# The output projection by seven half-size products, its first token half completed two products ahead, with norms by two and four tiles

## The chip, the cores and the metric

The kernel runs as one program on one core of a Trainium2 chip. The engines named here are PE (TensorE, matmuls; PEld is its weight load), DVE (VectorE), ACT (ScalarE), POOL (GpSimd) and SP (SyncE, which starts most transfers). The metric is the device time of one execution in microseconds. Three runs of the kernel before took 1897.14, 1898.09 and 1899.58 us; the median is 1898.09.

## The reference

A residual block over 1024 tokens of width 1024 in float32: two attention-like branches are merged by gates, projected by `w_out`, normalised and added to `x`; then comes an MLP with squared ReLU. The part around the change:

```python
merged = jax.nn.sigmoid(m_a) * y_a + jax.nn.sigmoid(m_d) * y_d
x = x + gate1 * rms_norm(merged @ w_out, post_mix_w)

h2 = rms_norm(x, pre_mlp_w) * (1.0 + scale2) + shift2
y = jnp.square(jax.nn.relu(h2 @ mlp_w1)) @ mlp_w2
x = x + gate2 * rms_norm(y, post_mlp_w)
```

`merged @ w_out` is 1024 x 1024 x 1024. Each RMS norm needs a sum of squares over all 1024 columns of a token, and `h2` is needed with features on the partitions, so that every token tile is transposed on PE.

## The kernel before

**Products in three matmuls.** A float32 operand is split into a high part (a cast, on ACT) and a low part (the difference, on DVE). A product is high x high, high x low and low x high: three matmuls of 128x128 by 128x512 for each 128 features.

**Seven products of halves.** The two branches' projections ahead of this stage are 1024-wide too, and each is done by seven products of half-size blocks (Strassen's way, with sums and differences of blocks formed on DVE). A half-size product is 4 token tiles x 4 feature tiles x 3 = 48 matmuls. The three of the branches are `ga`, `md` and `gd`; the reads of `gd`'s products in `gdn_read` finish the merged `z`, four tiles `zf(tb, kp)` for each half of the tokens with features on partitions. They need the gates from DRAM, loaded into tiles named `sl`.

**w_out before.** The eight token tiles are projected one after the other: for each, 8 feature tiles x 3 x 2 column halves = 48 matmuls into one `pm` tile (128x1024 in PSUM, two such in use by turns), 384 in all. `m_high`/`m_low` split the merged `z`; `wo_load`, `wo_high`, `wo_low` load and split `w_out`, whose low parts come for six of the eight feature tiles from a negated copy on ACT and an accumulating transfer that POOL starts.

**After a token tile** `token_chain` (lines 1794 to 1835) runs: ACT squares the `pm` tile with a sum into `cv`; DVE multiplies by the gain `gw1` into `z`; `norm1` is ten small operations on one column (a reciprocal root by iteration) and the residual into `xr`; ACT squares `xr`; `norm2` is again ten small operations and a scaling into `xh`; then `tr` has PE transpose `xh` in eight 128x128 pieces, by four into a `pa` tile, and ACT writes them, scaled and shifted, as `F`, the MLP's input.

**What sets the order.** A clock of ticks. In this stage a tick is six matmuls. `at(dt, fn)` puts a function on an agenda, due `dt` ticks ahead (`st` counts from the start of the branches), and `tick()` issues what is due behind the last matmul. After this each engine executes its instructions strictly in the order of issue (class `InOrder`, through whose `call` on line 38 they all go, so that every row of the profile shows L38 and tiles are told by their names). An instruction waits by semaphores for the tiles it touches; a write into a PSUM tile waits for earlier readers of that tile.

In `token_chain` `norm1` is due one tick after the tile, `norm2` four ticks, the output transfer six, the transposes nine and ten; the tile itself takes eight. Pass 1 of the MLP follows (`prod1`, 12 matmuls for each entry of `PASS1`); it needs `F` of the first half of the features split by `split_op`, and its weights' parts `w1`, prepared two entries ahead on ACT and DVE by `prep_pass1`. Sums of `F` for the second pass come through `todo`, filled 13 ticks into pass 1.

Of the kernel before, what the change touches and what calls it, by code (L numbers as in the profile page):

```python
# [8 lines left out]
F32 = mybir.dt.float32  # L9
# [41 lines left out]
def block_kernel(ctx: ExitStack, tc: tile.TileContext, x, c, ada_w, ada_b, pre_mix_w, post_mix_w,  # L51
# [1412 lines left out]
    def pair_tile(p, tag="w4", dt=F32):  # L1464
        return t4((128, 2, 512), dt, p, tag)
# [217 lines left out]

# [3 lines left out]
    def gdn_read(p, ps, h):  # L1687
# [5 lines left out]
        elif p == "P1":  # L1693
# [4 lines left out]
            at(13 - h, lambda: m_high(0, h))  # L1698
            at(16 - 3 * h, lambda: m_low(0, h))
        elif p == "P4":  # L1700
            s_ = gd.s.pop((1, 0, h))
            V.scalar_tensor_tensor(s_, s_, 1.0, pv, add, mul)
            z_add(0, 2 + h, s_)
            at(9 - 2 * h, lambda: m_high(0, 2 + h))
            at(14 - 3 * h, lambda: m_low(0, 2 + h))
        else:
            cb = int(p == "P5")
            y = u["P7" if cb else "P6", h]
            tt(V, y, pv, y, add)
            V.scalar_tensor_tensor(y, gd.s.pop((cb, 1, h)), 1.0, y, add, mul)  # L1710
            z_add(1, 2 * cb + h, y)
            n = 2 * (1 - cb) + h
            at((20, 20, 14, 12)[n], lambda: m_high(1, 2 * cb + h))
            at((22, 22, 16, 14)[n], lambda: m_low(1, 2 * cb + h))

    def branch(b, read):

        ps = None
        for p in ORDER:
# [7 lines left out]
    wo, wraw = [None] * 8, {}

    def wo_load(k, ring):
        if ring:  # L1730
            raw = rp.tile([128, 2, 1024], F32, tag="raw", name=nm("raw"))
            DMA.dma_start(raw, w_out[k * 128:(k + 2) * 128, :].rearrange("(k p) c -> p k c", p=128))
            wraw[k], wraw[k + 1] = raw[:, 0, :], raw[:, 1, :]
        else:
            for i in (k, k + 1):
                wraw[i] = t4(p="wor", tag="hd")
                DMA.dma_start(wraw[i], w_out[i * 128:(i + 1) * 128, :])

    def wo_high(k, tag):
        wo[k] = [t4((128, 1024), F32R, "wO", tag) for _ in range(2)]  # L1740
        A.copy(wo[k][0], wraw[k])

    def wo_low(k, dma=False):
        H, L = wo[k]
        if dma:
            A.activation(L, H.bitcast(F32), AF.Copy, scale=-1.0)
            G.dma_start(L, w_out[k * 128:(k + 1) * 128, :], accum_op=ALU.add)
        else:
            tt(V, L, wraw[k], H.bitcast(F32), sub)
# [44 lines left out]
    def token_chain(t, ps, xr):  # L1794

        hf, to = t // 4, slice(t % 4 * 128, t % 4 * 128 + 128)
        z, xh = t4(p="z", tag="hd"), t4(p="xh", tag="hd")
        v, v2 = small(1, "cv"), small(1, "cv")
        s = {}

        def norm1():
            V.tensor_scalar(v, v, 1.0 / D, 4 * EPS, ALU.mult, ALU.add)
            r = rsqrt(v, 1)
            V.scalar_tensor_tensor(xr, z, r, xr, ALU.mult, ALU.add)
            dump("x1", xr, lambda y: y[t * 128:(t + 1) * 128, :])
# [75 lines left out]


    xrs = {0: load_x(0)}
    for t in range(NT):
        hf, to = t // 4, (t % 4) * 128
        ps = pmt()
        if t + 1 < NT:
            at(7, lambda t=t: xrs.__setitem__(t + 1, load_x(t + 1)))
        if t == 4:
            load_pass1(0)
            load_pass1(1)
        if t == 5:  # L1900
            at(6, lambda: split_op("B11", F[0][0:2], (0,)))
            at(7, lambda: split_op("B11", F[0][0:2], (1,)))
            load_pass1(2)
            load_pass1(3)
        if t == 6:
            at(6, lambda: split_op("B21", F[0][2:4], (0,)))
        if t == 7:
            prep_pass1(0, 0, 3)
            prep_pass1(1, 0, 4)
            at(6, lambda: split_op("B21", F[0][2:4], (1,)))  # L1910
        for k in range(8):
            H, L = mH[k // 2][hf][:, k % 2, to:to + 128], mL[k // 2][hf][:, k % 2, to:to + 128]
            for (lh, w_) in ((H, 0), (H, 1), (L, 0)):
                for cf in range(2):
                    last["pe"] = T.matmul(ps[:, cf * 512:(cf + 1) * 512], lh, wo[k][w_][:, cf * 512:(cf + 1) * 512],
# [456 lines left out]
```

## Time and profile before

| what | value |
|---|---|
| time, median of 3 runs | 1898.09 us |
| the profiled execution's own time | 1896.27 us |
| its span | 1894.5 us |
| granted clock of TensorE, mean | 0.998 |
| first matmul on w_out | 1175.8 us into the span |
| last start of a matmul on w_out | 1268.3 us |
| transposes of `xh` | 64, from 1198.9 to 1283.9 us |
| DVE and ACT busy in 1176 to 1268.5 us | 62.5 and 43.3 us |

The profile is one execution. Its times are microseconds from the start of the span; a matmul's end is modelled, and matmuls overlap, so that the distance from one start to the next is what one costs. A row of the view by time gives start, duration, engine, line, operation, out<-in, shapes and count, and in brackets the engine's idle time ahead of it with what ended it. A row of groups gives the busy sum and the mean in ns after the bar. The view by tile gives smallest, median and largest duration in ns, and first and last start.

### The profile page before, as it was taken

What the parts mean: (1) busy time and instruction counts of PE and PEld (TensorE: products, weight loads), DVE (VectorE), ACT (ScalarE), POOL (GpSimd) and SP (SyncE); (2) the same over time, 40 slices, a digit from 0 to 9 for tenths busy, and PEclk for the clock granted to TensorE, in tenths of its full rate; (3) what the DMA queues carried; (4) which work ended last, traced back from release to release, by engine and by line L of the source; (5) the groups of instructions that cost most, each with busy time, mean ns of one, the idle gap of its engine ahead of it and who ended that gap; (6) DMA issues with size and microseconds to landing.
All of it is one profiled execution on the core that took longest, in us unless ns stands there. A gap on an engine that the chain in (4) does not pass through costs nothing.

```text
span 1894.5 us, 26553 instructions
## 1 busy us (share of the span) xinstructions
PE 1872.8 (99%) x10217; PEld 1572.3 (83%) x10217; DVE 1350.9 (71%) x2178; ACT 883.7 (47%) x1613; POOL 150.2 (8%) x140
## 2 busy tenths in 40 slices
PE   7999999999999999999999999999999999999998
PEld 5788888989898888888888888888888888888886
DVE  6664834968767666766788688666588777677887
ACT  5564324252332444444664556467544446433333
POOL 2120111010110000000101001000022220000001
PEclk9999999999999999999999999999999999999999
DMA  9695573223125444444868758336666768262425
GB/s 320 217 249 185 157 145 101 68 89 112 56 80 164 133 134 126 142 132 130 246 179 213 225 142 233 111 103 213 218 211 223 243 207 315 78 222 98 169 101 100
DMA packets 251567, 312.23 MB, mean 165 GB/s; under 512 B 72530, under 2 KB 178208, under 8 KB 251440
## 3 DMA queue, kind: packets, MB, share of 16 engines
q1 hardware_dynamic: 221936, 274.67, 45.3%
q0 software_dynamic: 13232, 20.85, 6.1%
q10 hardware_dynamic: 16272, 15.02, 2.4%
q8 instruction: 80, 1.31, 0.3%
q14 instruction: 47, 0.39, 0.1%
HBM read 230.10 MB, written 80.39 MB: 164 GB/s over the span
## 4 chain that ended last, share of the span: by engine, by line
PE 96%; DMA 1%; DVE 1%; ACT 1%; issue 0%; DVEq 0%; SPq 0%; ACTq 0%; POOLq 0%
PE pm L38 63%; PE pa L38 33%; DMA wq<-in_w_branch_gla_dram 1%; DMA x<-in_x_dram 0%; ACT hH L38 0%; ACT xT L38 0%; DVE rt L38 0%; ACT ob L38 0%; DVE ya L38 0%; DVE xT L38 0%; DVE rs L38 0%; ACT jk L38 0%; DVE hL L38 0%; DVE wL L38 0%; DVE raw L38 0%
## 5 line engine op out<-in xcount | busy, mean ns | idle before, releaser
L38 PE MATMUL pm<-hH,wH 128*128 128x512 f32 x864 | 286.3, 412 | 0.0
L38 PE MATMUL pm<-hL,wH 128*128 128x512 f32 x864 | 268.7, 392 | 0.0
L38 PE MATMUL pm<-hH,wL 128*128 128x512 f32 x864 | 267.2, 390 | 0.0
L38 PE MATMUL pm<-oH,wB 128*128 128x512 f32 x672 | 214.5, 394 | 0.0
L38 PE MATMUL pa<-w,yH 128*128 128x512 f32 (+1 forms) x696 | 212.3, 387 | 0.0
L38 PEld LDWEIGHTS pm<-hH,wL 128*128 128x128 f32 x864 | 162.1, 188 | 36.4
L38 PEld LDWEIGHTS pm<-hL,wH 128*128 128x128 f32 x864 | 162.2, 188 | 36.1
L38 DVE TENSOR_TENSOR w<-raw,w 128x512 fp32r<-128x512 f32 (+1 forms) x144 | 125.7, 875 | 49.6 <-ACT w L38 48.5
L38 PEld LDWEIGHTS pm<-hH,wH 128*128 128x128 f32 x864 | 145.1, 190 | 17.1 <-issue 0.2
L38 PEld LDWEIGHTS pa<-w,yH 128*128 128x128 f32 x696 | 130.1, 188 | 26.9 <-DVE ya L38 0.4
L38 PEld LDWEIGHTS pm<-oH,wB 128*128 128x128 f32 x672 | 126.2, 188 | 25.9 <-DMA wB<-in_w_branch_gla_dram 0.3
L38 ACT CAST w<-raw 128x512 fp32r<-128x512 f32 (+1 forms) x144 | 99.3, 711 | 89.3 <-DVE raw L38 79.5
L38 PE MATMUL pa<-w,yL 128*128 128x512 f32 (+1 forms) x348 | 134.5, 387 | 0.0
L38 PE MATMUL pm<-oL,wB 128*128 128x512 f32 x336 | 130.9, 390 | 0.0
L38 PE MATMUL pa<-oB,w 128*128 128x512 f32 x480 | 111.4, 390 | 0.0
L38 ACT CAST wH<-raw 128x1024 fp32r<-128x1024 f32 x62 | 64.5, 1048 | 98.1 <-PE pm L38 55.8
L38 PEld LDWEIGHTS pa<-oB,w 128*128 128x128 f32 x480 | 89.8, 188 | 18.5
L38 DVE SCALAR_TENSOR_TENSOR cv<-pm,ccol,cv 128x1023 f32<-128x1023 f32 (+2 forms) x72 | 92.1, 1279 | 13.4 <-ACT cv L38 12.0
L38 DVE TENSOR_TENSOR wL<-raw,wH 128x1024 fp32r<-128x1024 f32 x62 | 75.3, 1219 | 34.6 <-ACT wH L38 34.5
L38 PE MATMUL pm<-oT,w 128*128 128x512 f32 x384 | 90.8, 389 | 0.0
L38 PE MATMUL pa<-oT,w 128*128 128x512 f32 x384 | 90.8, 389 | 0.0
L38 DVE TENSOR_TENSOR ya<-pa,ya 128x512 f32<-128x512 f32 (+1 forms) x83 | 55.9, 682 | 43.7 <-PE pa L38 43.7
(378 smaller groups left out, 3701.1 us busy)
## 6 DMA issues: line engine op xcount, KB each, us to landing
yL<-y_d SPq DMA_DIRECT2D x53, 512.0 KB, 7.6
raw<-in_mlp_w_dram SPq DMA_DIRECT2D x23, 1024.0 KB, 6.2
raw<-in_w_in_dram SPq DMA_DIRECT2D x18, 1024.0 KB, 7.2
raw<-in_w_in_dram SPq DMA_DIRECT2D x32, 512.0 KB, 4.9
araw<-in_ada_w_dram SPq DMA_DIRECT2D x32, 512.0 KB, 3.8
raw<-in_mlp_w_dram SPq DMA_DIRECT2D x18, 512.0 KB, 5.1
araw<-in_ada_w_dram SPq DMA_DIRECT2D x32, 256.0 KB, 6.5
sl<-sg_d SPq DMA_DIRECT2D x16, 512.0 KB, 8.9
```

The costliest lines, as they stand in the source:

```text
L38: r = fn(*args, **kw)
```

## The change

The projection becomes seven half-size products, P2, P1, P6, P5, P3, P7, P4, of 48 matmuls or eight ticks each, over halves of tokens, features and columns; 336 matmuls. `out_product` runs one: four token tiles j, each with four feature tiles. P2 has its own two `pm` tiles; P1, P6, P5 and P3 accumulate onto a second pair, read in between by `copy_y` or `first_half`; P7 and P4 accumulate in four `pa` tiles, with `add_y` after each. A `pm` tile now holds the 512 columns of two token tiles. Tokens 0 to 511 are complete after P3 (tick 40 of the stage), tokens 512 to 1023 after P4 (tick 56).

The loads and sums of blocks stand in a table with ticks (`out_plan`), and all low parts are made on DVE. `token_chain` is gone. `square` works on 128x512; the gain is multiplied on DVE for the first half's second columns (`second_half`) and on POOL for the rest (`weigh`). `norm1` takes two tiles at a time in the first half (ticks 38 and 42) and four in the second (64), `norm2` likewise (42 and 47; 71). `turn` has PE transpose two tiles in pieces, eight into a `pm` tile, and ACT writes `F` in operations of 128x256. The second half's norms and transposes lie in pass 1. On SP the gain `gw` is now loaded behind the first two `xr`.

```diff
+    def out_product(p, ps, start):
+        for j in range(4):
+            c_ = slice(j * 128, j * 128 + 128)
+            for k in range(4):
+                (xH, xL), (wH, wL) = wx[p, k // 2], ww[p, k // 2]
+                mmc(ps[j], xH[:, k % 2, c_], wH[:, k % 2], start and k == 0, False, not start)
+                mmc(ps[j], xH[:, k % 2, c_], wL[:, k % 2], False, False, not start)
+                mmc(ps[j], xL[:, k % 2, c_], wH[:, k % 2], False, k == 3, not start)
+                if k % 2:
+                    tick()
...
-    def token_chain(t, ps, xr):
...
-        A.activation(xh, ps, AF.Square, accum_out=v)
-        tt(V, z, ps, gw1, mul)
-        at(1, norm1)
-        at(3, lambda: A.activation(z, xr, AF.Square, accum_out=v2))
-        at(4, norm2)
-        at(6, lambda: LD.dma_start(out[t * 128:(t + 1) * 128, :], xr))
-        at(9, lambda: tr(0))
-        at(10, lambda: tr(1))
...
+    def norm1(hf, a, n):
+        v = small(n, "cv")
+        tt(V, v, va[hf][:, a:a + n], va[hf][:, 4 + a:4 + a + n], add)
+        V.tensor_scalar(v, v, 1.0 / D, 4 * EPS, ALU.mult, ALU.add)
+        rn[hf, a] = rsqrt(v, n)
...
+    def second_half(j, ps):
+        square(0, 1, j, ps)
+        if j % 2 == 0:
+            Y[0, 1, j // 2] = pair_tile("y", "hd")
+        tt(V, Y[0, 1, j // 2][:, j % 2], ps, gw1[:, HALF[1]], mul)
...
+    for a, t in ((0, 38), (2, 42)):
+        on(t, lambda a=a: (norm1(0, a, 2), residual(0, a, a), residual(0, a + 1, a)))
+    for a, t in ((0, 40), (2, 45)):
+        on(t, lambda a=a: square2(0, a))
+        on(t + 1, lambda a=a: square2(0, a + 1))
+    for a, t in ((0, 42), (2, 47)):
+        on(t, lambda a=a: norm2(0, a, 2))
+    for a, t in ((0, 45), (2, 51)):
+        for g in range(2):
+            on(t + g, lambda a=a, g=g: turn(0, a, g))
...
+    on(64, lambda: norm1(1, 0, 4))
+    for j in range(4):
+        on(64 + j, lambda j=j: residual(1, j, 0))
+        on(66 + j, lambda j=j: square2(1, j))
+    on(71, lambda: norm2(1, 0, 4))
+    for n in range(4):
+        on(74 + n, lambda n=n: turn(1, n // 2 * 2, n % 2))
...
+        for j in range(4):
+            if p == "P3":
+                at(3 + 2 * j, lambda j=j, ps=psb: second_half(j, four(ps)[j]))
+            elif p in ("P7", "P4"):
+                at(3 + 2 * j, lambda j=j, ps=psc, c=int(p == "P7"): add_y((1, c, j // 2), j, ps[j]))
...
-    at(13, lambda: todo.extend(t_ops()))
+    at(23, lambda: todo.extend(t_ops()))
...
-        if n < 24:
+        if n < 30:
```

How this stands on the engines, at three places.

PE at a change of token tile. Before, the second tile's last matmuls (`pm2865`) and the third tile's first (`pm2888`, another buffer):

```order
L38 MATMUL pm2865_10612<-wO2847_10522,mH2833_10448 128x512 x2
L38 MATMUL pm2865_10612<-wO2848_10523,mH2833_10448 128x512 x2
L38 MATMUL pm2865_10612<-wO2847_10522,mL2842_10489 128x512 x2
L38 MATMUL pm2888_10709<-wO2818_10384,mH2776_10212 128x512 [waits DVE_49]
L38 MATMUL pm2888_10709<-wO2818_10384,mH2776_10212 128x512
L38 MATMUL pm2888_10709<-wO2819_10385,mH2776_10212 128x512 x2
```

Now, in P3, the token tile j = 1 into `pm2959`, whose other half is the finished j = 0:

```order
L38 MATMUL pm2959_10612<-wO2989_10774,mH2980_10727 128x512
L38 MATMUL pm2959_10612<-wO2990_10775,mH2980_10727 128x512
L38 MATMUL pm2959_10612<-wO2989_10774,mL2981_10728 128x512
L38 MATMUL pm2959_10612<-wO2994_10790,mH2982_10739 128x512 [waits DVE_49]
L38 MATMUL pm2959_10612<-wO2995_10791,mH2982_10739 128x512
L38 MATMUL pm2959_10612<-wO2994_10790,mL2983_10740 128x512
L38 MATMUL pm2959_10612<-wO2994_10790,mH2982_10739 128x512
```

The fourth of these rows is the seventh matmul of j = 1; its wait is for DVE's product `y` of j = 0, issued one tick into j = 1, which in turn waits for ACT's square. In j = 3 the seventh matmul into `pm2960` carries the same wait, for the product of j = 2. Before, the wait stood at the first matmul of a tile, for a reader two tiles back.

DVE around these products. Before, between the second norm of the first token tile (`xh2856`) and the first norm of the second tile, which begins with `cv2880`:

```order
L38 SCALAR_TENSOR_TENSOR rt2873_10659<-rt2873_10659,cv2858_10609 128x1 [waits DVE_49]
L38 SCALAR_TENSOR_TENSOR rs2872_10658<-rt2873_10659,rs2872_10658 128x1 [waits DVE_49]
L38 TENSOR_SCALAR xh2856_10607<-xr2849_10549,rs2872_10658 128x1024 [waits DVE_49]
L38 TENSOR_TENSOR mL2875_10678<-U2490_8992,mH2871_10648 128x1024
L38 TENSOR_TENSOR mL2876_10693<-U2521_9144,mH2874_10676 128x1024 [waits Activation_49]
L38 TENSOR_TENSOR z2878_10703<-pm2865_10612,gw12720_9965 128x1024 [waits Activation_49]
L38 TENSOR_SCALAR cv2880_10705<-cv2880_10705 128x1
```

Now, from the end of the first norm of two tiles (`rs3016`) by the four residual halves (`xr`), the products of j = 2 and j = 3 (`y3022`) and a low part of `w_out` (`wO`) to the start of the next norm (`cv3037`):

```order
L38 SCALAR_TENSOR_TENSOR rs3016_10901<-rt3017_10902,rs3016_10901 128x2 [waits DVE_49]
L38 SCALAR_TENSOR_TENSOR xr2954_10590<-y2950_10577,rs3016_10901,xr2954_10590 128x512 [waits DMAHW0_49,DVE_49,Pool_49]
L38 SCALAR_TENSOR_TENSOR xr2954_10590<-y3013_10875,rs3016_10901,xr2954_10590 128x512
L38 SCALAR_TENSOR_TENSOR xr2958_10610<-y2950_10577,rs3016_10901,xr2958_10610 128x512 [waits DMAHW1_49]
L38 SCALAR_TENSOR_TENSOR xr2958_10610<-y3013_10875,rs3016_10901,xr2958_10610 128x512
L38 TENSOR_TENSOR y3022_10927<-pm2960_10613,gw12778_9965 128x512 [waits DVE_49,Activation_49]
L38 TENSOR_TENSOR y3022_10927<-pm2960_10613,gw12778_9965 128x512 [waits Activation_49]
L38 TENSOR_TENSOR wO3033_10952<-wq2848_10298,wO3032_10951 128x1024
L38 TENSOR_TENSOR cv3037_10968<-va2884_10502 128x2
L38 TENSOR_SCALAR cv3037_10968<-cv3037_10968 128x2 [waits DVE_49]
```

The product for which PE waits in j = 3 now stands behind a norm and four residual halves of the tiles before, and the scaling `xh` of the first two tiles (some 25 rows further) behind the next norm and its four residual halves too.

PE at the first transposes. Before, the first token tile's `xh2856` is transposed one tick into the third tile, four pieces to a `pa` tile:

```order
L38 MATMUL pm2888_10709<-wO2818_10384,mH2776_10212 128x512
L38 MATMUL pm2888_10709<-wO2819_10385,mH2776_10212 128x512 x2
L38 MATMUL pm2888_10709<-wO2818_10384,mL2780_10240 128x512 x2
L38 MATMUL pa2891_10718<-ident_95,xh2856_10607 128x128 [waits DVE_49]
L38 MATMUL pa2891_10718<-ident_95,xh2856_10607 128x128 x3
L38 MATMUL pm2888_10709<-wO2820_10396,mH2776_10212 128x512 x2
L38 MATMUL pm2888_10709<-wO2821_10397,mH2776_10212 128x512 x2
```

Now, 30 matmuls into P7 (`pa` tiles), the first two tiles by turns:

```order
L38 MATMUL pa3026_10943<-wO3007_10851,mH2985_10765 128x512
L38 MATMUL pa3026_10943<-wO3008_10852,mH2985_10765 128x512
L38 MATMUL pa3026_10943<-wO3007_10851,mL2986_10766 128x512
L38 MATMUL pm3045_11024<-ident_95,xh3012_10873 128x128 [waits DVE_49]
L38 MATMUL pm3045_11024<-ident_95,xh3014_10889 128x128 [waits DVE_49]
L38 MATMUL pm3045_11024<-ident_95,xh3012_10873 128x128
L38 MATMUL pm3045_11024<-ident_95,xh3014_10889 128x128
```

The transposes of a tile came nine ticks after its last matmul; those of j = 0 and 1 now come eleven and nine ticks after theirs, and wait for both scalings.

More of the change, by code (lines that the diff above doesn't have):

```diff
@@ L1723, in branch @@
             for h in range(2):
-                at(5 + 4 * h + (4 if b is gd and p == "P3" and h else 0), lambda p=p, ps=ps, h=h: read(p, ps, h))
+                at(5 + 4 * h, lambda p=p, ps=ps, h=h: read(p, ps, h))
             b.product(p, ps, start)
[L1727 to L1749, printed above, removed]
+    wx, ww, bq = {}, {}, {}
+    B11, B12, B21, B22 = (0, 0), (0, 1), (1, 0), (1, 1)
+    def wo_ring(kp):
+        raw = rp.tile([128, 2, 1024], F32, tag="raw", name=nm("raw"))
+        DMA.dma_start(raw, w_out[kp * 256:(kp + 1) * 256, :].rearrange("(k p) c -> p k c", p=128))
+        bq[B11, kp], bq[B12, kp] = raw[:, :, HALF[0]], raw[:, :, HALF[1]]
@@ L1832, in load_x, with square @@
-    def load_x(t):
-        xr = t4(p="xr", tag="sl")
-        LD.dma_start(xr, x[t * 128:(t + 1) * 128, :])
-        return xr
+    va, vb = [small(8, "va") for _ in range(2)], [small(4, "vb") for _ in range(2)]
+    Y, xrs, xhs = {}, {}, {}
+    def load_x(t):
+        xrs[t] = t4(p="xr", tag="sl" if t % 4 < 2 else "w4")
+        LD.dma_start(xrs[t], x[t * 128:(t + 1) * 128, :])
+    def square(hf, c, j, src):
+        if c == 0 and hf == 0:
+            out_ = Y["jk"][:, j % 2]
+        else:
+            if 4 * hf + j not in xhs:
+                xhs[4 * hf + j] = t4(p="xh")
+            out_ = xhs[4 * hf + j][:, HALF[c]]
+        A.activation(out_, src, AF.Square, accum_out=va[hf][:, 4 * c + j:4 * c + j + 1])
@@ L1888, in prep_pass1 @@
         at(dt + 1, lambda: w_low(w1[g, k], src))
[L1891 to L1915, printed above, removed]
-                                          start=(k == 0 and w_ == 0 and lh is H), stop=(k == 7 and lh is L)).ins
-            tick()
-        token_chain(t, ps, xrs.pop(t))
@@ new lines, in block_kernel, with on, four, copy_y @@
+    base = clock[0]
+    def on(t, fn):
+        at(base + t - clock[0], fn)
+    def four(ps):
+        return [ps[j // 2][:, HALF[j % 2]] for j in range(4)]
+    def copy_y(key, ps):
+        y = Y[key] = pair_tile("y")
+        A.copy(y, r2(ps))
+    def add_y(key, j, ps):
+        y = Y[key][:, j % 2]
+        tt(V, y, ps, y, add)
+    def first_half(h, ps):
+        tt(V, Y[0, 0, h], r2(ps), Y[0, 0, h], add)
+    def second_half(j, ps):
[3 more added lines that the diff above has]
+        tt(V, Y[0, 1, j // 2][:, j % 2], ps, gw1[:, HALF[1]], mul)
@@ new lines, in block_kernel @@
+    for n, (c, h) in enumerate(((1, 0), (1, 1), (0, 0), (0, 1))):
+        on((56, 57, 59, 60)[n], lambda c=c, h=h: [square(1, c, 2 * h + e, Y[1, c, h][:, e]) for e in range(2)])
+        on((57, 58, 60, 61)[n], lambda c=c, h=h: weigh(1, c, h))
+    on(64, lambda: norm1(1, 0, 4))
[5 more added lines that the diff above has]
+        on(74 + n, lambda n=n: turn(1, n // 2 * 2, n % 2))
```

152 lines of the change are left out of this document (106 added, 46 removed).

## The prediction

> **What bounds the kernel now.** I read the page's busy times and its chain of work first, then the waits of TensorE (PE), and then the w_out stage alone.
>
> ```profile
> PE 1872.8 (99%) x10217; PEld 1572.3 (83%) x10217; DVE 1350.9 (71%) x2178; ACT 883.7 (47%) x1613; POOL 150.2 (8%) x140
> PE 96%; DMA 1%; DVE 1%; ACT 1%; issue 0%; DVEq 0%; SPq 0%; ACTq 0%; POOLq 0%
> ```
>
> PE is busy for 99% of the span and carries 96% of the chain that ends last. The table of what PE waited for has seven rows; these are its first two, the others are no longer:
>
> ```profile
> PE pm L38 <- DVE x L38: 10.1, 1, 10.1
> PE pm L38 <- ACT hH L38: 0.6, 1, 0.6
> ```
>
> The 10.1 us are the start of the program. So a matmul removed is worth its slot, and a wait added to PE costs its length. The stage itself:
>
> ```profile
> 1176.00:1222.00 46.00, 46.00 (x212) 38.08 (x212) 31.62 (x80) 17.90 (x34) 0.00 (x0) 1.00 0.39 125
> 1222.00:1268.50 46.50, 46.50 (x222) 38.54 (x221) 30.84 (x98) 25.43 (x54) 0.00 (x0) 1.00 0.39 125
> ```
>
> The columns are PE, PEld, DVE, ACT and POOL busy, then the granted clock. PE has no gap in 92.5 us; DVE has about a third of the time free, at full clock.
>
> **What is removed: 48 matmuls.**
>
> ```profile
> L38 PE MATMUL pm<-wO,mH x256: 389/389/478, 1175.8 to 1267.9; 128*128 128x512 f32 x128
> L38 PE MATMUL pm<-wO,mL x128: 387/389/397, 1176.7 to 1268.3; 128*128 128x512 f32 x128
> ...
> 1175.81 1.07 PE L38 MATMUL pm<-wO,mH 128*128 128x512 f32 x4
> 1176.72 0.62 PE L38 MATMUL pm<-wO,mL 128*128 128x512 f32 x2
> 1177.17 0.39 PE L38 MATMUL pm<-wO,mH 128*128 128x512 f32 x1
> ```
>
> A matmul lasts 389 ns but overlaps the next; the price is the step. Six of them, one tick, take 1177.17 - 1175.81 = 1.36 us, 0.2267 us each. There are 256 + 128 = 384 before and 7 x 48 = 336 after, of the same shape. That is 48 x 0.2267 = **-10.9 us**, the whole gain there can be. The transposes are 64 of 128x128 in both.
>
> **What is added: three waits of PE behind the third accumulated product.** Before, a token tile had its own `pm` tile and a long time. The chain of one tile:
>
> ```profile
> 1208.95 0.61 PE L38 MATMUL pm<-wO,mL 128*128 128x512 f32 x2
> 1209.40 1.07 PE L38 MATMUL pm<-wO,mH 128*128 128x512 f32 x4
> ...
> 1222.59 0.60 PE L38 MATMUL pa<-ident,xh 128*128 128x128 f32 x4
> ```
>
> ```profile
> 1209.60 1.03 ACT L38 ACTIVATE xh<-pm 128x1024 f32<-128x1024 f32 x1 [5.10 <-PE pm L38]
> 1210.52 0.19 ACT L38 ACTIVATION_READ_ACCUMULATOR xh<-pm 128x1 f32 x1
> ...
> 1215.18 1.06 ACT L38 ACTIVATE z<-xr 128x1024 f32<-128x1024 f32 x1 [0.45 <-DVE xr L38]
> ```
>
> ```profile
> 1210.75 1.23 DVE L38 TENSOR_TENSOR z<-pm,gw 128x1024 f32<-128x1024 f32 x1 [3.54 <-ACT xh L38]
> 1211.89 0.14 DVE L38 TENSOR_SCALAR cv<-cv 128x1 f32<-128x1 f32 x1
> ...
> 1213.81 1.28 DVE L38 SCALAR_TENSOR_TENSOR xr<-z,rs,xr 128x1024 f32<-128x1024 f32 x1
> 1216.37 0.15 DVE L38 TENSOR_SCALAR cv<-cv 128x1 f32<-128x1 f32 x1 [1.28 <-ACT z L38]
> ...
> 1218.29 0.75 DVE L38 TENSOR_SCALAR xh<-xr,rs 128x1024 f32<-128x1024 f32 x1
> ```
>
> What to see: the square starts 0.20 us after the tile's last matmul slot (1209.60 against 1209.40); its accumulator read ends 0.08 us after it; the DVE product follows 0.04 later; ten small norm operations take 1213.81 - 1211.89 = 1.92 us, 0.192 each; `xh` is done at 1219.04, and PE asks for it at 1222.59. So 3.5 us were spare. For the halves of the new order:
>
> ```profile
> L38 ACT ACTIVATE uy<-pa 128x512 f32<-128x512 f32 x16 | 9.6, 599 | 14.0 <-PE pa L38 14.0
> L38 DVE TENSOR_TENSOR y<-pm,uy 128x512 f32<-128x512 f32 x16 | 11.0, 686 | 5.6 <-PE pm L38 5.6
> ...
> 1889.97 1.42 DVE L38 SCALAR_TENSOR_TENSOR xr<-yg,rs,xr 128x512 f32<-128x512 f32 x2
> ```
>
> A square of 512 columns is taken at 0.60 us, a product from PSUM at 0.69 (the next operation can start after about 0.60), a residual half at 0.75 with a step of 1.42 - 0.75 = 0.67.
>
> In P3 one `pm` tile holds two token tiles (j = 0, 1 and j = 2, 3), and `second_half(j)` is issued one tick into j+1. The rows shown with the change have PE's next matmul into that `pm` tile wait for this read, though it writes the other half. Behind the waiting matmul the whole of PE is queued.
>
> *Wait 1, in j = 1.* The square begins only when the tick just before has drained: 0.20 + 0.60 + 0.08 + 0.04 + 0.69 = **1.6 us**, nothing lies beside it.
>
> *Wait 2, in j = 3.* Call the end of j = 1 A. DVE then has the product of j = 1 (can start at A + 0.92, next at A + 1.52), eleven small operations (2.11, to A + 3.63), four residual halves (3 x 0.67 + 0.75, to A + 6.39), and only then the product of j = 2, done at A + 7.1. PE has 18 matmuls, 4.08 us. Wait: **3.0 us**.
>
> *Wait 3, at the first transposes, 30 matmuls into P7.* P3 ends at A + 7.1 + 1.36 = A + 8.5, PE arrives at A + 15.3. DVE, from A + 8.5: square and hand-over 0.92, product 0.60, a low part of w_out (1.13 by the step of 2.35 us for two, in the last fence of DVE rows below), second norm 2.11, four residual halves 2.68, norm2 of the first two tiles 1.92, two scalings (0.75, then a step of about 0.67): `xh` of the second tile at A + 19.3. The transposes take the two tiles by turns, so the wait is **4.0 us**. Before, 3.5 us were spare here; now norm1 and residuals of the next two tiles stand ahead in DVE's queue.
>
> **What is moved off TensorE's path.** Later transposes of the first half and the start of pass 1 come after PE has lost these 8.6 us, and DVE has caught up: I take them at nothing, with about 1 us of cover. The second half's chain lies in pass 1. There DVE has between P4's end and the first weight behind norm2: two adds into `y` and eight weight low parts of 512 columns (10 x 0.69), three low parts of 1024 (3 x 1.13), the two norms (2.11 + 1.92), eight residual halves (8 x 0.67) and four scalings (4 x 0.7), some 22.5 us. PE gives it 18 ticks and eight transposes, 25.2 us. But norm2 must wait for ACT's fourth square, and ACT's squares stand in a row with the copies of pass 1's own results, which follow PE's ticks: some 3.5 us of DVE's time are lost there by the same sums, and the weight comes about 1 us late. I take **1.0 us** and bounds of 0 and 3, the latter if three of the four squares (1.06 in the fence) cost their place. Multiplying by the gain on POOL is covered even at the slower of
>
> ```profile
> L38 POOL TENSOR_TENSOR go<-go,rs 128x1024 f32<-128x1024 f32 x8 | 15.0, 1894 | 156.2 <-DVE rs L38 156.2
> L38 POOL TENSOR_TENSOR zm<-zm,b 128x1024 f32<-128x1024 f32 x4 | 12.6, 3149 | 28.1 <-ACT b L38 28.1
> ```
>
> because three at 3.15 us end 9.5 us after tick 57, and the residual that needs them comes after tick 64 and a norm; the cover ends at about 3.7 us each. The six accumulating transfers that go from POOL's queue hid under PE already: nothing. On SP, `gw` now stands behind two `xr` loads that wait for the merge's last reads of `sl`; it is issued near tick 14, POOL wants it at 16, DVE's product at 35, 26 us later, against at most
>
> ```profile
> DMA to landing us min/median/max: 3.7/8.9/16.8
> ```
>
> of a tile of the same size. If POOL starts late, its result is still wanted only at tick 38. ACT's F operations, 16 wide ones for 64, and the later sums for pass 1 (tick 23 for 13) lie beside matmuls: nothing, cover a pass long.
>
> One more place is open, the start. With 24 matmuls to each `pm` tile of P2, PE needs the second tile at tick 4, 1181.25, after the merge's last read of the same buffer. Before:
>
> ```profile
> 1175.82 1.23 DVE L38 SCALAR_TENSOR_TENSOR U<-sl,U 128x1024 f32<-128x1024 f32 x1 [3.54 <-DMA sl<-sg_d]
> ...
> 1178.22 2.35 DVE L38 TENSOR_TENSOR wO<-raw,wO 128x1024 fp32r<-128x1024 f32 x2
> 1180.49 1.22 DVE L38 TENSOR_TENSOR U<-pm,U 128x1024 f32<-128x1024 f32 x1
> ```
>
> DVE stood for 3.5 us for a transfer. If it lands as late again, the new queue (an add, a low part of w_out, one of P1's left side, a difference, then the read) frees the tile at about 1183.0: 1.75 us. If it lands 2 us earlier, now that the accumulating transfers are gone from the same stretch, nothing. I take nothing.
>
> **Sum:** -10.9 + 1.6 + 3.0 + 4.0 + 1.0 = -1.3 us. The profiled execution took 1896.27 us (span 1894.5), 1.8 under the median 1898.09, so I expect 1895.0 for a like execution and **1896.8** for the median. Hand-overs from DVE to PE that no row prices may add 0 to 0.2 at each of three waits (0.20 is PE to ACT), so this case runs from 1894.5 to 1899.5. A measurement of this kernel can tell 0.2% (3.8 us) from no change; this is inside.
>
> **Rivals.**
> *A, the matmuls' whole gain.* If the reads of a `pm` half did not hold PE, or DVE's queue ran shorter, up to -10.9 remains: 1887.2; with only the third wait left, made longer by what the other two no longer hide, 1890 to 1893. For it: DVE idles a third of this stage. Against it: the waits stand in the program, and each chain is serial, so idle time elsewhere on DVE doesn't shorten it. 0.22.
>
> *B, a slow TensorE after a long wait, which ends on the slower side.* After its 10.06 us without work PE ran the same transposes at half pace at first:
>
> ```profile
> 10.06 1.09 PE L38 MATMUL pm<-ident,x 128*128 128x128 f32 x4 [10.06 <-DVE x L38]
> 10.94 0.85 PE L38 MATMUL pa<-ident,x 128*128 128x128 f32 x3
> ...
> 13.07 1.87 PE L38 MATMUL pa<-ident 128*128 128x128 f32 x12
> 14.78 0.25 PE L38 MATMUL pa<-ident,vt 95*128 95x95 f32 x1
> ...
> 15.39 0.60 PE L38 MATMUL pm<-ident,x 128*128 128x128 f32 x4
> 15.83 0.49 PE L38 MATMUL pa<-ident,x 128*128 128x128 f32 x3
> ...
> 28.45 2.56 PE L38 MATMUL pm<-hH,w 128*128 128x512 f32 x10 [0.63 <-ACT hH L38]
> ```
>
> Four took 10.94 - 10.06 = 0.88 us, later 15.83 - 15.39 = 0.44, by the starts of the next rows; the twelve from 13.07 took 1.71, so the pace changed near 14.1. Half pace for 4.1 us loses 2.05 us. The granted clock reads 1.00 throughout and doesn't show it. After 0.63 us of waiting nothing of the kind is seen (ten matmuls in 2.56 us). The deciding length lies between 0.63 and 10.06; waits 2 and 3 have 3.0 and 4.0. One loss gives 1898.9; two, if DVE gains nothing from the slower PE, 1900.9; I put B at 1899.9, and up to 1902.7 with the wait at the start. 0.18. The Trainium skill, "TensorE: Matmul & The Clock Gate", Part 1, says that the clock halves after about one idle window, some 3.4 us, free-running, and that about as long a busy stretch restores it; the trace agrees with the length of recovery (4.1 us), and no run here shows a wait between 0.63 and 10.06. By that figure wait 3 alone may cross it, for an estimate of 1.7 us, 1898.5.
>
> *C, the late transfer at the start:* 1896.8 + 1.75 = 1898.6. For it: it was late before. Against it: fewer transfers beside it. 0.10.
>
> The forecast keeps 0.50. The range reaches into A and over most of B, 1890.5 to 1902; it leaves out the full gain of A and the sum of all lateness. **Faster** by over 0.2% (under 1894.3): A and the lower edge of the forecast, 0.25. **Slower** by over 0.2% (over 1901.9): B with another loss, 0.12, and 0.05 of the others, 0.17. **Same**: 0.58.
>
> **What would show it.** PE's waits after: `pm` waiting for DVE `y` twice, 1.6 and 3.0 us, some 48 and 55 us after the first w_out matmul (210 and 234 steps, and the first wait), and PE waiting for DVE `xh` for some 4 us; the stage's PE time 10.9 us less without them; a weight wait of about 1 us in pass 1. A `pm` wait near 1181 is C. A step of 0.45 us between matmuls after a wait is B. I am wrong in mechanism if these waits are under 1 us, or if waits appear behind P1 or P6, whose first reads I take to have 1.4 us of cover.

## The result, and the profile after

| | before | after |
|---|---|---|
| time, median (lowest to highest; 4 runs each) | 1898.61 us (1897.14 to 1899.58) | 1912.77 us (1910.94 to 1914.99) |
| the profiled execution, its span | 1896.27, 1894.5 us | 1912.39, 1910.6 us |
| mean granted clock | 0.998 | 0.995 |

The change makes the kernel slower, by a ratio of 1.0076 with a 95% interval from 1.0058 to 1.0093. That is 14.2 us between the medians, where a change of 1.3 us in the other direction was forecast. The first line of the page of after, engines with busy time, share of the span and instructions:

```profile
PE 1871.3 (98%) x10169; PEld 1567.8 (82%) x10169; DVE 1386.7 (73%) x2129; ACT 887.3 (46%) x1609; POOL 163.0 (9%) x140
```

The 48 matmuls are gone (10217 less 10169), which at 0.2267 us are 10.9 us. Yet PE's busy time is only 1.5 us lower: matmuls at half clock count as busy for twice as long (5.1 us more), and the restarts after waits (2.2 us) and some 2 us ahead of the stage, both below, count as busy too. DVE has 49 instructions fewer and 35.8 us more to do. The table of what PE waited for in after, with the sum, the number and the longest:

```profile
PE pm L38 <- DVE x L38: 9.9, 1, 9.9
PE pm L38 <- DVE y L38: 6.1, 3, 3.1
PE pa L38 <- DVE w L38: 5.0, 2, 4.5
PE pm L38 <- DVE xh L38: 3.4, 2, 3.1
PE pm L38 <- ACT y L38: 1.3, 1, 1.3
PE pm L38 <- DVE U L38: 1.1, 1, 1.1
```

The first is the start of the program, as before. The other five are new. In the view by time, PE of after, the rows with these waits (in brackets the idle time ahead and what ended it), with two rows that show the restart, and the first matmul behind the stage:

```profile
1178.12 0.62 PE L38 MATMUL pm<-wO,mH 128*128 128x512 f32 x2
...
1183.33 0.39 PE L38 MATMUL pm<-wO,mL 128*128 128x512 f32 x1
1184.81 0.73 PE L38 MATMUL pm<-wO,mH 128*128 128x512 f32 x2 [1.09 <-DVE U L38]
1185.37 0.40 PE L38 MATMUL pm<-wO,mL 128*128 128x512 f32 x1
...
1197.32 0.73 PE L38 MATMUL pm<-wO,mH 128*128 128x512 f32 x2 [1.34 <-ACT y L38]
...
1232.47 0.74 PE L38 MATMUL pm<-wO,mH 128*128 128x512 f32 x2 [1.74 <-DVE y L38]
...
1241.34 1.22 PE L38 MATMUL pm<-wO,mH 128*128 128x512 f32 x2 [3.09 <-DVE y L38]
...
1254.44 0.33 PE L38 MATMUL pm<-ident,xh 128*128 128x128 f32 x1 [3.05 <-DVE xh L38]
...
1285.68 20.79 PE L38 MATMUL pa<-oB,w 128*128 128x512 f32 x82 [4.49 <-DVE w L38]
...
1373.29 2.88 PE L38 MATMUL pm<-oT,w 128*128 128x512 f32 x12
```

1232.47, 1241.34 and 1254.44 are the three waits that the prediction named, at 1.74, 3.09 and 3.05 us plus 0.33 for the second tile. The rows at 1184.81 and 1197.32, and a third of 1.28 us at 1204.36, lie in P2, in P1 and at the start of P6, where it had none; the last wait, in pass 1, is 4.5 us where it had 1.0.

**The budget of the stage.** From the first `w_out` matmul to the first matmul that reads `oT`, after takes 1373.29 - 1178.12 = 195.2 us; before it took from 1175.81 to 1357.49, 181.7. The difference of 13.5 us is made up of -10.9 for the matmuls; 16.9 for the idle time in brackets (three early waits 3.7, P3 4.8, `xh` 3.4, pass 1 5.0); some 2.2 for eight restarts; and 5.1 for half clock, below. That is 13.3. A restart costs what the bracket doesn't show. The bracket counts from a matmul's modelled end, 1183.33 + 0.39, while its slot ends at 1183.33 + 0.23, which is 0.16 earlier; and the first two matmuls take 1185.37 - 1184.81 = 0.56 where 0.45 is usual. Together that is 0.27 us each.

The remaining 2.3 us of the profiled run lie ahead of the stage, whose first matmul came at 1178.12 for 1175.81. It came anywhere from 1176.5 to 1179.7 us in the profiles of the changed kernels. Little of it is waiting: PE's idle time ahead of the stage is 13.0 us for 12.7. What sets it I have not settled.

**Why the early waits.** The view by windows, columns PE, PEld, DVE, ACT, POOL busy, then the granted clock; first before, then after:

```profile
1178.00:1231.00 53.00, 53.00 (x247) 43.89 (x246) 35.98 (x102) 21.76 (x44) 0.00 (x0) 1.00 0.40 129
1178.00:1275.00 97.00, 97.00 (x457) 80.34 (x456) 65.37 (x191) 48.25 (x100) 0.00 (x0) 1.00 0.35 114
```

```profile
1178.00:1231.00 53.00, 49.02 (x212) 39.00 (x210) 52.90 (x44) 27.22 (x34) 5.76 (x2) 1.00 0.15 51
1178.00:1275.00 97.00, 85.07 (x370) 68.35 (x369) 80.08 (x114) 47.76 (x73) 5.76 (x2) 0.96 0.28 93
```

From 1178 to 1231 DVE is busy for 52.90 of 53 us, where it had 17 us free before. It is the bound there (f1 and g1 below test this), and PE waits for whatever stands at the end of its queue, be it `U`, `y`, or ACT's copy `y`, which stands behind a cast that itself waited for DVE. From 1231 to 1275 DVE is not full: 80.08 - 52.90 = 27.2 of 44 us.

Some 3.7 us of the 52.90 are not the change's own work. POOL multiplies the first half's gain there, and two low parts beside it take 6.03 us for 2.35:

```profile
1209.08 5.76 POOL L38 TENSOR_TENSOR y<-y,gw 128x1024 f32<-128x1024 f32 x2 [102.61 <-DMA gw<-gw_d]
1209.89 6.03 DVE L38 TENSOR_TENSOR wO<-raw,wO 128x1024 fp32r<-128x1024 f32 x2
```

The three early waits had ended by then.

**Why the wait in pass 1.** DVE of after around POOL's products, and POOL:

```profile
1274.62 1.22 DVE L38 TENSOR_TENSOR oB<-F,oB 128x1024 fp32r<-128x1024 f32 x1
1275.75 0.68 DVE L38 TENSOR_TENSOR y<-pa,y 128x512 f32<-128x512 f32 x1
1276.35 6.51 DVE L38 TENSOR_TENSOR oB<-F,oB 128x1024 fp32r<-128x1024 f32 x2
1282.79 0.68 DVE L38 TENSOR_TENSOR y<-pa,y 128x512 f32<-128x512 f32 x1
1283.39 5.61 DVE L38 TENSOR_TENSOR w<-raw,w 128x512 fp32r<-128x512 f32 x3
```

```profile
1276.04 2.41 POOL L38 TENSOR_TENSOR y<-y,gw 128x1024 f32<-128x1024 f32 x1 [61.21 <-ACT xh L38]
1278.73 9.12 POOL L38 TENSOR_TENSOR y<-y,gw 128x1024 f32<-128x1024 f32 x3 [0.28 <-ACT xh L38]
```

A low part `oB` takes 1.22 us at 1274.62, and two take 6.51 us at 1276.35, while POOL runs. The add `y`, with one operand from PSUM, takes 0.68 us beside POOL as well. So POOL's four products, 2.41 us for the first and 9.12 for the other three, were "covered" on POOL, but made DVE's queue longer, and the weight part `w` that PE wants at 1281.2 comes out 4.5 us late. The Trainium skill, "GPSIMD Engine Reference", section 1 (Specifications), says that POOL's interfaces to SBUF are shared with VectorE, with contention for DVE instructions that have two SBUF inputs; the trace agrees, and the prediction had not weighed it.

**Half clock.** The windows of after around the wait that ended at 1241.34:

```profile
1240.00:1242.00 2.00, 0.66 (x2) 0.57 (x3) 1.18 (x2) 2.00 (x4) 0.00 (x0) 0.83 0.95 389
1242.00:1244.00 2.00, 2.00 (x6) 1.60 (x5) 0.00 (x0) 0.38 (x2) 0.00 (x0) 0.50 0.33 135
1244.00:1246.00 2.00, 2.00 (x9) 1.58 (x8) 0.98 (x2) 1.63 (x3) 0.00 (x0) 0.82 0.00 0
```

The granted clock is 0.50 in the second, and the three lose 2 x (0.17 + 0.50 + 0.18) = 1.7 us. The same sum stands behind the waits of 3.05 and 4.49 us: 5.1 us in all. Behind 1.09, 1.34, 1.28 and 1.74 us the clock stays at 1.00.

### The profile page after: what moved, and what is told of

Its sections match the earlier page's. It is cut to its first block, busy times and chain, and to the rows that moved or that the text cites. A ratio compares the mean times of both kernels' runs of the same rounds, so it can differ in the third digit from the quotient of the medians.

```text
span 1910.6 us, 26421 instructions
## 1 busy us (share of the span) xinstructions
PE 1871.3 (98%) x10169; PEld 1567.8 (82%) x10169; DVE 1386.7 (73%) x2129; ACT 887.3 (46%) x1609; POOL 163.0 (9%) x140
## 5 line engine op out<-in xcount | busy, mean ns | idle before, releaser
L38 DVE TENSOR_TENSOR wL<-raw,wH 128x1024 fp32r<-128x1024 f32 x62 | 76.1, 1231 | 34.8 <-ACT wH L38 34.7
```

The source lines that it names most:

```text
L38: r = fn(*args, **kw)
```

## The experiments

Two theories were set against each other at each place: that a named chain or a place in the order makes PE wait, or that DVE has more work than time, so that a wait that is taken away comes back elsewhere. Each ratio is to the kernel before, run on the same chip at the same time; after, e1 to e4, e5 with f1 and f2, f3, and g1 with g2 ran apart, so between these groups the ratios compare better than the medians.

| run | median, us | ratio to before (95%) | what is different |
|---|---|---|---|
| after | 1912.77 | 1.0076 (1.0058 to 1.0093) | |
| e1_gain_dve | 1905.47 | 1.0040 (1.0026 to 1.0055) | gains of the second half on DVE |
| e2_reads_late | 1910.83 | 1.0071 (1.0056 to 1.0086) | P3's reads behind whole `pm` tiles |
| e3_order | 1911.70 | 1.0073 (1.0058 to 1.0088) | low parts of P1 and P6 later |
| e4_gain_out | 1905.31 | 1.0042 (1.0027 to 1.0057) | no gain in the second half |
| e5_before_pool | 1899.21 | one run | before, with four adds on POOL |
| f1_low_dma | 1900.45 | 1.0014 (1.0004 to 1.0023) | e1, six low parts off DVE |
| f2_low_dma_reads | 1900.98 | 1.0014 (1.0004 to 1.0023) | f1, a new order |
| f3_moved | 1892.28 | 0.9968 (0.9956 to 0.9980) | f2, seven steps moved |
| g1_no_dma | 1896.63 | 0.9994 (0.9984 to 1.0004) | f3, low parts back on DVE |
| g2_gain_pool | 1894.36 | 0.9980 (0.9971 to 0.9990) | f3, all gains back on POOL |

### The gain: POOL, DVE, or none (e1, e4, e5)

```diff
-        tt(G, y, y, gw1[:, HALF[c]].unsqueeze(1).to_broadcast([128, 2, 512]), mul)
+        tt(V if hf else G, y, y, gw1[:, HALF[c]].unsqueeze(1).to_broadcast([128, 2, 512]), mul)
```

> The changed kernel with the second half's gain multiplied on DVE instead of POOL (four products of 128x1024 in pass 1). Theory POOL-holds-DVE: while POOL multiplies, DVE's operations beside it last 2 to 3 us instead of 0.69 or 1.22; on DVE the four cost 4 x 1.13 = 4.5 us but the others keep their length, so the 4.49 us wait of PE for a weight in pass 1 falls to 1 to 2 us and the half clock behind it (1.7 us) goes: about 1908 us against 1912.8. Rival, DVE's queue alone is too long: 4.5 us more on it make the wait about 9 us: 1915 to 1918.

In e4 the second half's gain is left out, so that tokens 512 to 1023 lack that factor:

```diff
-        on((57, 58, 60, 61)[n], lambda c=c, h=h: weigh(1, c, h))
```

> The changed kernel without the second half's multiplication by the gain (the four POOL products of pass 1 are left out, so tokens 512 to 1023 lack it). Theory POOL-holds-DVE: the 4.49 us wait in pass 1 falls below 1 us and the half clock behind it goes: 1906 to 1907 us, and DVE's low parts beside it last 1.22 and 0.69 us. Rival, DVE's own queue: the wait stays at 3 to 4.5 us and the time at 1911 to 1913.

DVE of e1, the same low parts and a gain product that now stands between them:

```profile
1275.02 2.35 DVE L38 TENSOR_TENSOR oB<-F,oB 128x1024 fp32r<-128x1024 f32 x2
1277.29 1.22 DVE L38 TENSOR_TENSOR y<-y,gw 128x1024 f32<-128x1024 f32 x1
```

Two low parts take 2.35 us for 6.51. DVE does POOL's four products itself, 4.9 us of work, and is done earlier all the same. The wait in pass 1 falls from 5.0 to 0.5 us, and the median by 7.3 us (6.8 by the ratios). e4, with the products nowhere, gains no more than e1 (1905.31 against 1905.47). So what the gain on POOL cost here was that POOL held DVE up; on DVE the product costs PE nothing that these runs show. Part of the gain is half clock, 1.7 us lost in e1 for 5.1: the wait in pass 1 is gone, and that for `xh` came out at 2.1 us at most, with no slow stretch behind it.

The cost by itself, in the kernel before, where four adds of the merge go from DVE to POOL:

```diff
-            z_add(1, 2 * cb + h, y)
+            tt(G, zf(1, 2 * cb + h), zf(1, 2 * cb + h), y, add)
```

> The kernel before with four of its additions of 128x1024 (the last tiles of the merged z) on POOL instead of DVE. Theory POOL-holds-DVE: POOL's additions last 2.4 to 3.1 us where DVE works beside them, and DVE's operations beside them 2 to 3.4 us instead of 1.22; where DVE idles POOL's take 1.9. The time stays within 3 us of before. Rival, the two engines do not hinder each other: DVE's stay at 1.22 us.

POOL, then DVE, of this run:

```profile
1167.59 3.31 POOL L38 TENSOR_TENSOR U<-U,U 128x1024 f32<-128x1024 f32 x1
...
1181.34 2.38 POOL L38 TENSOR_TENSOR U<-U,U 128x1024 f32<-128x1024 f32 x1 [3.56 <-DVE U L38]
```

```profile
1167.42 4.56 DVE L38 TENSOR_TENSOR mL<-z,mH 128x1024 fp32r<-128x1024 f32 x2
```

Beside POOL's add, two low parts take 4.56 us on DVE; undisturbed they take 2.35. POOL pays as well: 3.31 us beside DVE's work, 2.38 at 1181.34, where DVE idles. This is in the kernel before, so it belongs to the two engines and not to the new order.

### P3's two reads (e2)

```diff
-                at(3 + 2 * j, lambda j=j, ps=psb: second_half(j, four(ps)[j]))
+                at(5 + 4 * (j // 2), lambda j=j, ps=psb: second_half(j, four(ps)[j]))
```

Both reads of a `pm` tile come behind its last matmul, and no matmul of P3 has to wait for one.

> The changed kernel with the reads of P3's columns issued one tick after both token tiles of a pm tile are complete (ticks 5, 5, 9, 9 instead of 3, 5, 7, 9). Theory tile-wait: PE's two waits for DVE y inside P3 (1.74 and 3.09 us) vanish, with one half-clock stretch (1.7 us); the wait for xh in P7 grows from 3.4 to about 6.5 us, since the chain now ends later against PE: about 1909 us. Rival, DVE is simply full: the wait for xh takes over all that was saved (8 us and more) and the time stays at 1912 to 1914.

The longest wait of PE in e2:

```profile
1252.66 0.48 PE L38 MATMUL pm<-ident,xh 128*128 128x128 f32 x1 [8.91 <-DVE xh L38]
```

P3's 4.8 us are gone, and the wait for `xh` grows from 3.05 to 8.91 us. The median falls by 1.9 us at most, within the two intervals. The waits in P3 were real, but with the reads moved alone PE loses their time at the transposes, behind a chain that ends later. This isn't a full DVE, the rival's reason. DVE of e2 at the product of j = 2:

```profile
1241.80 0.69 DVE L38 TENSOR_TENSOR y<-pm,gw 128x512 f32<-128x512 f32 x1 [2.50 <-ACT xh L38]
```

DVE stood 2.50 us for ACT's square. The chain to `xh` goes to and fro between ACT and DVE, and each waits for the other.

### The order of the early low parts (e3)

```diff
-                   (-3 + 4 * kp, b_cast, "P1", B11, kp), (-2 + 4 * kp, b_low, "P1", B11, kp),
-                   (-4 + kp, a_cast, "P1", Z11, kp), (-3 + kp, a_low, "P1", Z11, kp),
+                   (-3 + 4 * kp, b_cast, "P1", B11, kp), (2 + kp, b_low, "P1", B11, kp),
+                   (-4 + kp, a_cast, "P1", Z11, kp), (2 + kp, a_low, "P1", Z11, kp),
...
-                   (9 + kp, b_cast, "P6", "t2", kp), (10 + kp, b_low, "P6", "t2", kp),
+                   (10 + kp, b_cast, "P6", "t2", kp), (13 + kp, b_low, "P6", "t2", kp),
```

> The changed kernel with P1's low parts (weights of kp 0 and left side) issued at ticks 2 and 3 instead of before the stage, and P6's weight casts one tick later, behind the copy of P2's second tile. Theory order: PE's three early waits (1.09 for DVE U, 1.34 for ACT y, 1.28 for DVE y) shrink to under 1 us in all: about 1909 us. Rival, DVE is full from 1178 to 1231: the wait at tick 4 goes, but as much reappears at P1's first matmuls or at P6's first tile: 1911.5 to 1914.

PE of e3 in the same stretch:

```profile
1198.02 0.73 PE L38 MATMUL pm<-wO,mH 128*128 128x512 f32 x2 [1.84 <-ACT y L38]
...
1205.15 0.70 PE L38 MATMUL pm<-wO,mH 128*128 128x512 f32 x2 [1.39 <-DVE y L38]
...
1207.32 0.50 PE L38 MATMUL pm<-wO,mH 128*128 128x512 f32 x1 [0.32 <-DVE wO L38]
...
1211.87 0.73 PE L38 MATMUL pm<-wO,mH 128*128 128x512 f32 x2 [0.38 <-DVE y L38]
```

The wait in P2 is gone. The next is 1.84 us for 1.34, the one after 1.39 for 1.28, and two small ones are new: 3.9 us for 3.7. DVE is still busy for 52.80 of the 53 us from 1178. This order only moves the waits, as the rival had it; that no order could help is not shown by one.

### Taking work from DVE (f1), and then the order (f2, f3)

f1 is e1 with the low parts of `w_out` for P2, P1 and P3 made as before the change, by a negated copy on ACT and an accumulating transfer from POOL's queue:

```diff
+        if p in ("P2", "P1", "P3"):
+            H, L = ww[p, kp]
+            A.activation(L, H.bitcast(F32), AF.Copy, scale=-1.0)
+            G.dma_start(L, w_out[key[0] * 512 + kp * 256:key[0] * 512 + kp * 256 + 256, HALF[key[1]]].rearrange("(k p) c -> p k c", p=128), accum_op=ALU.add)
+            return
```

> e1_gain_dve, and the low parts of w_out's unsummed blocks (six of 128x1024, for P2, P1 and P3) made as before the change, by a negated copy on ACT and an accumulating transfer: 6 x 1.13 = 6.8 us less for DVE, four of them ahead of tick 9. Theory DVE-is-full: PE's waits at ticks 4, 14 and 16 (1.10, 1.34, 1.28 us) shrink to under 1 us in all and the stage gains 3 to 4 us: 1901 to 1902.5. Rival, they are fixed by the order of ACT's and DVE's queues, not by DVE's load: 1905 again, or later where a transfer lands late.

Six operations of 1.22 us leave DVE. All three early waits go with them, and the ratio falls from 1.0040 to 1.0014. In P3 and at the transposes PE still waits 1.50, 3.08 and 2.1 us, so there it is the chain and not DVE's load that makes it wait.

f2 changes the order on top: P3's reads as in e2, the first norm and the squares at other ticks, transposes and some splits later, all gains on DVE.

```diff
-    for a, t in ((0, 38), (2, 42)):
+    for a, t in ((0, 38), (2, 43)):
...
-    for a, t in ((0, 40), (2, 45)):
+    for a, t in ((0, 39), (2, 45)):
...
-    for a, t in ((0, 45), (2, 51)):
+    for a, t in ((0, 46), (2, 53)):
```

> f1_low_dma, and in P3 the reads after a pair of token tiles (ticks 37 and 41), norm2 of the first two tiles ahead of norm1 of the next two, first transposes at ticks 46 and 47 for 45 and 46, the next two tiles' at 53 and 55 for 51 and 52, all gains on DVE. Theory: no PE wait inside P3, under 1 us at the first transposes, 0 to 2 us at the second ones or at the start of pass 1, no wait over 2.8 us and so no half clock: about 1892, faster than before by some 5 us. Rival, DVE is still full through P7 and P4, and what goes in P3 comes back as one wait of 5 us or more with a half clock: 1897 to 1901.

This missed: 1900.98 us, no better than f1. DVE of f2, then PE:

```profile
1205.58 1.22 DVE L38 TENSOR_TENSOR y<-y,gw 128x1024 f32<-128x1024 f32 x1 [1.52 <-DMA gw<-gw_d]
```

```profile
1209.13 0.73 PE L38 MATMUL pm<-wO,mH 128*128 128x512 f32 x2 [2.69 <-DVE y L38]
```

The first half's gain products had gone to DVE at the tick at which they stood on POOL. There DVE, which executes in order, stood 1.52 us for the late load of `gw`, and PE waited 2.69 us behind it, with a slow stretch after that. In after POOL had stood for the same load, and no row of PE waits for that product. f3 moves this product to ticks 28 and 30 (from 16 and 20), and six more steps by one to five ticks, among them the squares and gains of P7, which come earlier:

```diff
-        on(16 + 4 * h, lambda h=h: weigh(0, 0, h))
-    for a, t in ((0, 38), (2, 43)):
+        on(28 + 2 * h, lambda h=h: weigh(0, 0, h))
+    for a, t in ((0, 37), (2, 42)):
...
-                at(5 + 4 * (j // 2), lambda j=j, ps=psb: second_half(j, four(ps)[j]))
+                at(4 + 4 * (j // 2), lambda j=j, ps=psb: second_half(j, four(ps)[j]))
```

> f2_low_dma_reads with DVE's first gain products moved from ticks 16 and 20 to 28 and 30 (there they stood for gw's transfer ahead of a read for which PE waited 2.69 us), the reads in P3 right behind the second token tile of a pair (ticks 36 and 40) with the chain behind them one tick earlier, and P7's squares and gains moved from pass 1 into P4 (ticks 51 to 55). Theory queue-order: the 2.69 us wait with its half clock (1.7 us) goes, the wait for xh falls from 2.1 to under 1 us and the waits in pass 1 from 1.8 to 1 us: 1893 to 1896, faster than before. Rival, DVE is full: they reappear as waits of like length elsewhere: 1899 to 1901.

The waits of PE in f3, and the windows:

```profile
PE pm L38 <- DVE x L38: 10.1, 1, 10.1
PE pm L38 <- DVE xh L38: 1.1, 2, 0.8
PE pa L38 <- DVE y L38: 0.9, 1, 0.9
```

```profile
1178.00:1231.00 53.00, 53.00 (x234) 43.32 (x233) 47.22 (x52) 29.96 (x39) 3.61 (x3) 1.00 0.46 106
1231.00:1275.00 44.00, 41.31 (x194) 33.18 (x193) 37.40 (x83) 30.32 (x62) 0.00 (x0) 1.00 0.49 161
```

PE has no gap in the first stretch, DVE has 5.8 us free there, and no wait is long enough for the clock to fall. At 1892.28 us this beats both kernels: 0.9968 of before.

### f3 with one thing put back (g1, g2)

g1 has the six low parts on DVE again (the added lines of f1 taken out), with all else as in f3.

> f3_moved with the six low parts of w_out's unsummed blocks back on DVE (6.8 us more for it). Theory DVE-is-full: between 1178 and 1231 there is no room for them, PE's early waits come back (3 to 5 us in all, some with a half clock): 1896 to 1899. Rival, only the order mattered: 1892 to 1893.5.

```diff
-        tt(V, y, y, gw1[:, HALF[c]].unsqueeze(1).to_broadcast([128, 2, 512]), mul)
+        tt(G, y, y, gw1[:, HALF[c]].unsqueeze(1).to_broadcast([128, 2, 512]), mul)
```

That is g2, with all gain products on POOL.

> f3_moved with all six gain products on POOL as in the change. Theory POOL-holds-DVE: POOL's products last 2.4 to 3.3 us, DVE's operations beside them stretch by 1 to 2.2 us for each product, more than the 1.13 that a product costs on DVE itself, and PE waits for weights or reads in P4 and pass 1: 1895 to 1898. Rival, POOL takes 6.8 us off a full DVE: 1890 to 1892.

PE of g1, the early waits:

```profile
1184.80 0.73 PE L38 MATMUL pm<-wO,mH 128*128 128x512 f32 x2 [1.09 <-DVE U L38]
...
1197.31 0.73 PE L38 MATMUL pm<-wO,mH 128*128 128x512 f32 x2 [1.34 <-ACT y L38]
```

They are back to the hundredth, with the third of 1.29 us, in a kernel whose later order is quite another; windows show DVE at 52.29 of 53 us. It costs 4.4 us (1896.63 against 1892.28; 4.9 by the ratios), which is the three waits, 3.7, and their restarts. g2 costs some 2 us (1894.36), less than I had expected, and its interval overlaps f3's. POOL and DVE of g2:

```profile
1252.62 5.23 POOL L38 TENSOR_TENSOR y<-y,gw 128x1024 f32<-128x1024 f32 x2 [31.58 <-ACT xh L38]
```

```profile
1253.81 1.77 DVE L38 TENSOR_TENSOR w<-raw,w 128x512 fp32r<-128x512 f32 x1
1255.51 0.68 DVE L38 TENSOR_TENSOR y<-pa,y 128x512 f32<-128x512 f32 x1
```

Beside POOL DVE's weight part takes 1.77 us, alone 0.69; the add from PSUM is untouched. The mechanism is there, but the products stand some ticks earlier, and no wait of PE for a weight is above 0.5 us; that DVE had time to spare there is the likely reason, not a tested one. So 7 us was the price at that place in the order, not of the edit as such.

## Why the prediction was wrong, step by step

**The matmuls: right.** 48 fewer, at 0.2267 us. f3 gets 6.3 of the 10.9 us (1898.57 against 1892.28).

**The three waits behind P3: right in place and cause, and nearly in size.**

| wait | forecast | measured |
|---|---|---|
| P3, j = 1 | 1.6 | 1.74 |
| P3, j = 3 | 3.0 | 3.09 |
| first `xh` | 4.0 | 3.38 |
| pass 1 | 1.0 (0 to 3) | 4.96 |
| the start, P1 and P6 | 0 (1.75 in one rival) | 3.71 in three |
| restarts | 0 to 0.2 at three waits | 0.27 at eight, 2.2 |
| half clock | rival, 2.05 once or twice | 1.7 three times, 5.1 |

Adding up a serial chain by rows of before gave the two waits in P3 to within 0.2 us. Even with DVE relieved, in f1, they stay at 1.50 and 3.08 us. The third was 0.6 under its forecast in after, and about 2.5 us in e1 and e3. That difference comes from the clock. DVE's product of j = 3, in after and then in e1:

```profile
1245.02 0.69 DVE L38 TENSOR_TENSOR y<-pm,gw 128x512 f32<-128x512 f32 x1 [3.74 <-ACT xh L38]
```

```profile
1245.25 0.69 DVE L38 TENSOR_TENSOR y<-pm,gw 128x512 f32<-128x512 f32 x1 [2.82 <-ACT xh L38]
```

In after the clock fell as PE resumed, at 1241.3; P3's last six matmuls ran at half pace, and the square behind them, with the whole chain to `xh`, came 0.92 us later than in e1, where the clock fell 1.1 us after PE had resumed. The wait for the first `xh` is longer by as much, 3.05 for 2.12 us.

**The step that failed** is that the early part of the stage was put at nothing. For the start the prediction says "I take nothing", and to the first reads behind P1 and P6 it gives "1.4 us of cover". At the start it went through DVE's queue, but charged it only if a transfer landed late; the transfer was in time, and the queue alone cost 1.09 us. It had read "DVE has about a third of the time free, at full clock" from the windows of before, and never summed DVE's work after over these first 40 ticks. It is 14.7 us more from 1178 to 1275 (80.08 against 65.37, 3.7 of it POOL's doing), in fewer and larger operations, and fills the first 53 us. The three waits that came of it took 3.71 us. The prediction itself named waits behind P1 or P6 as the sign of being wrong in mechanism, and they came. f1 and g1 show that six low parts of 1.22 us decide these waits; e3's other order only moved them. The rival C asked for the right place with the wrong cause: the wait at 1184.81 is not for a late `sl`, since DVE had no idle time ahead of it from 1159 on.

**Pass 1** was mis-sized by 4 us because the gain product was priced on POOL alone ("covered even at the slower of"). What it takes from DVE's speed stood in no term. e1, e4 and e5 show it.

**The rival B** was right in kind and near in price (1.7 us for 2.05), and went with the forecast's own waits rather than against them: waits 2 and 3 each caused it, and so did pass 1. With its half clock at the two long waits counted in the sum, the forecast would have been 3.4 us higher; that alone doesn't reach the result. The granted clock, which had read 1.00 in the slow start of before, shows these stretches at 0.50. Of the 14.8 us between the forecast for this stage (-1.3) and what it took (+13.5), 3.7 are the early waits, 4.0 pass 1, 5.1 half clock and some 2 the restarts; `xh` gave 0.6 back. The forecast's lower edge of 1894.5 does not follow from its terms, which give 1895.8 with nothing for pass 1.

**Open.** The 2.3 us ahead of the stage. Separate `pm` tiles for the token tiles of P3, which would take away those waits without moving the reads, were not tried.

## What to carry to other kernels

Before a change is costed by the chains it makes, sum its work for each engine over the stage: an engine at two thirds that is given 15 us more in 97 may be full in the part that matters, and then a wait removed there by order comes back at the next tile. Where the engine has time and PE waits all the same, it is a chain, and there the order helped (f2 and f3). An element-wise operation moved to POOL is not free while DVE works on operands in SBUF: charge DVE for it, and put it where DVE idles or reads PSUM. And a wait of some 3 us cost PE about half as much again in slow matmuls here, 1.7 us, and 3.1 us in f1, while waits up to 2.2 us cost nothing of the kind; two waits of 1.5 are better than one of 3.

## What the runs showed of the hardware

**POOL and DVE slow each other.** DVE 128x1024 with both operands in SBUF: 1.22 us alone, 2.3 (e5) to 3.3 (after) beside a POOL operation on SBUF; 128x512, 0.69 alone and 1.77 beside it (g2). POOL's own add of 128x1024 takes 2.38 alone and 3.31 beside DVE (e5). With one operand from PSUM, DVE keeps its 0.68.

**The clock after a wait.** In all profiles here, no wait of up to 2.2 us was followed by half pace, and waits of 2.69 (f2), 2.83 (e4), 3.05 and more were. The length of the wait is not the whole of it. Read in windows of half a microsecond, the clock of after falls at 1241.30, 1254.95 and 1285.67 and rises 3.4 us later each time. The falls are 13.65 and 30.72 us apart, four and nine times 3.41; in e4 two are 13.65 apart, in e2 two are 37.54, eleven times 3.41. So in these runs the clock changes only at the ends of cells of 3.41 us, and what counts looks to be PE's idle time within one cell. In e1 a fall at 1243.60 followed 2.30 us of idle time in its cell, of a wait of 3.09; in e2 a fall at 1245.94 followed 2.19. The wait of 1.84 us in e3, which by an estimate lay in one (fourteen cells of 3.41 back from that run's fall at 1243.97), was followed by none. Each run has its cells elsewhere, so how much of a wait falls into one is luck.

A cell with idle time left in it can also fail to bring the clock back. In f1, after a wait of 3.08 that ended at 1237.70, the whole stretch reads

```profile
1231.00:1246.00 15.00, 11.92 (x40) 9.21 (x40) 9.99 (x31) 5.69 (x12) 0.00 (x0) 0.77 0.40 126
```

and 15 x 0.23 x 2 = 6.9 us are at half clock, two cells, from 1237.10 to 1243.93. The first still held 0.60 us of the wait. Some 3.1 us are lost, where after lost 1.7 behind the same wait. The Trainium skill, "TensorE: Matmul & The Clock Gate", Part 1, has the clock halve after one idle window of some 3.4 us, free-running, and recover after as long a busy time; the traces agree on the window and the recovery, but a window need not be idle throughout: 2.19 us of it were enough in e2.
